# Zeros for the blocks' DRAM tiles come from a constant; attention's output is split between filling pieces

## The chip, the cores and the metric

The kernel runs on one core of one Trainium2 chip. The metric is device time in microseconds (us), the median of three runs. A core has TensorE (PE) for matmuls, with its weight loads (PEld) beside them, VectorE (DVE) and ScalarE (ACT) for elementwise work, GpSimd (POOL), and SyncE (SP), whose queue issues every DMA of this kernel in the order in which they stand in it. Each engine works through its own queue in order and waits on semaphores for what the others produce.

## The reference

One layer of a hybrid block over 256 latent tokens and 256 context tokens, width 2048:

```
sh, sc, g = modulation(cond)                     # silu(cond) @ w_mod + b_mod, for latents and for context
u  = (rmsnorm(x) * (1 + sc) + sh) @ w_in         # one wide projection, its columns are cut into branches
# branch 1: RWKV-7 time mixing, 16 heads of 64, two directions, context first, then latents
#           S = S*w + (S @ -kk) x akk + v x k ;  y = S @ r        (a recurrence over the tokens)
# branch 2: latent attention, 8 heads: softmax(q k^T) v, times silu(zm)
out = x + g * ((g_r * (o_rwkv @ w_br_r) + g_m * (o_mla @ w_br_m)) @ w_out)
```

The recurrence is computed in chunks of 64 tokens, and each chunk needs the inverse of a triangular 64x64 matrix. The inverse of its four 16x16 blocks on the diagonal is computed apart, on 64 partitions, so these blocks travel through DRAM: out of a tile of the chunk, into a narrow tile, and back into a wide one whose other entries must be zero.

## The kernel before

**Precision.** A float32 operand is split into a high part, rounded by ScalarE (`hi`), and a low part, subtracted by VectorE (`lo = src - hi`); a product is three matmuls, `hi*hi`, `hi*lo`, `lo*hi` (`mm3`, L254). `split` (L218) is this pair of operations. Weights come in pieces of 128x512 float32 (`piece`, L234, whose DMA is L237), are split by `parts_of` (L240) and are used by twelve matmuls each. Nearly all elementwise operations are recorded by the profile under one line, L142, and nearly all matmuls under L115, L117 or L120, so groups are told apart by their tiles.

**Stage 1** (to about 136 us): for 16 slices `k` of the width, the modulation weights `wm` (4 x 512 KB for each slice, L296, in 11 buffers), the projection's first six column tiles (`w` from `w_first`, 2 x 192 KB), their splits and their matmuls into the tiles `a`. PE, ACT and DVE have their order written out by hand here (`manual_schedule`).

**Stage 2** (to about 880 us): the recurrence. A main chain of small matmuls runs through `front`, `diagonal` and `back` for each pair of heads. Beside it a generator, `bg`, issues filling pieces: projections of other columns (`proj_g`, L414; weights from `w_proj`), and the matmuls of the output gate on `w_mod_g` (`gate_mm`, L442). A planner in Python (`drive`, L549), which adds up estimated costs of matmuls and elementwise operations, decides after which step of the chain a filling piece is written. DMAs and GpSimd's operations have no cost in it.

**The zeros.** Each of two DRAM tiles, `dw0` and `dw1` (2x8x2x4160 float32), takes the inverted diagonal blocks for a group of heads, and is read back as the wide 64x64 matrices into `WT`. All that isn't a diagonal block has to be zero, and is written once, before stage 2. GpSimd sets the SBUF tile `WT0` to zero (L598), and four DMAs copy it out (L603 and L604, 512 KB and 8 KB for each tile). `WT0` lies in the pool `rw`, in memory that stage 1's pool `p1` used, so the memset waits until that stage's last loads and operations have let go of it. The four DMAs stand in SP's queue between the first two pieces of `w_proj` and the next ones.

**Stage 3** (to about 1117 us): attention, head by head (`attend`, L1362), with filling pieces between its steps; its output is collected in `omla` (128x8x256). The filling pieces here are `branch_g` (L1417), the recurrence's output times `w_br`: for each of 16 column tiles `j` it loads two pieces of weights and a gate tile `th` from DRAM (L1423), does 2 x 12 matmuls into a tile `acc` (two buffers in PSUM), multiplies `acc` by the gate into `th` on VectorE (L1429), which frees `acc`, and stores `th` (L1430). After the last head, `omla` is split into `obh` and `obl` in two halves of 128x1024 (L1452 to L1454). Then twelve steps of `bg` are taken, the pieces' buffers move to the pool `mg`, which is deeper, and the rest of `bg` is run out (L1463). A branch takes three steps of `bg`: one for each piece and one for its end.

**Stage 4** (from about 1117 us): attention's output (`obh`, `obl`) times the other half of `w_br`, into `chp`, merged with the gates, then `w_out`.

**The order on each engine** follows from the code's order by a rule. When the kernel is built, a list scheduler goes through modelled time, and each engine, when it is free, takes from its ready instructions the one that was written first. An instruction that isn't ready is passed over. `high_priority(HP)` in `parts_of` puts the splits of weights 500 places ahead. The order found in this way is then fixed; on the chip each engine keeps to it and waits where its operands aren't there.

Of the kernel before, what the change touches and what calls it, by code (L numbers as in the profile page):

```python
# [16 lines left out]
P = 128  # L17
# [5 lines left out]
CH = 64  # L23
# [7 lines left out]
_CW = [("ident", 128), ("ones", 2), ("mq", 128), ("mr", 128),  # L31
       ("zoff", 128), ("bones", 128), ("hsel", 2),
       ("hmean", 2), ("sel2", 2)]
# [5 lines left out]
NCONST = _o  # L39
# [15 lines left out]
BEHIND = mybir.DependencyInfo(mybir.DependencyClass.NoSync, mybir.DependencyReason.DATA)  # L55
# [6 lines left out]
PD = CH * CH + CH  # L62
# [84 lines left out]
def hybrid_block(  # L147
# [20 lines left out]
    nc = tc.nc  # L168
# [10 lines left out]
    cc = cst.tile([P, NCONST], F32, name="cc")  # L179
    vv = cst.tile([P, NVEC], F32, name="vv")  # L180
    nc.sync.dma_start(vv, vecs)
    nc.sync.dma_start(cc, consts)

    def con(name):
        o, w = CO[name]
# [2 lines left out]
    def vec(name, i, n=1):  # L188
        o, w = VO[name]
        return vv[:, o + i:o + i + n]  # L190
# [27 lines left out]
    def split(src, hi, lo):  # L218

        S.copy(hi, src)  # L220
        V.tensor_tensor(lo, src, hi.bitcast(F32), ALU.subtract)

    def halfs(pool, shape, name, bufs=2):
        return [pool.tile(shape, F32R, name=name + c, tag=name + c, bufs=bufs) for c in "hl"]
# [51 lines left out]
    with tc.tile_pool(name="p1", bufs=2) as p1:  # L276
# [11 lines left out]
        V.memset(ssil, 0.0)  # L288
        V.tensor_scalar(ssil[:, 0:2 * KT], st, 0.5, None, ALU.mult)

        parts, mods = {}, {}

        def load_mod(k):
            for r in range(4):
                wm = p1.tile([P, 4, 256], F32, name="wm", tag="wm", bufs=NWM)
                nc.sync.dma_start(wm, w_mod_ss[k, r])  # L296
                yield wm

        def mod_a(k):

            pm = pp.tile([P, 512], F32, name="pm", tag="ch")
            for r, wm in enumerate(load_mod(k)):
                for g in range(4):
                    k0 = 2 * (4 * r + g)
                    E.matmul(pm[32 * g:32 * g + 32, 0:256], lhsT=ssil[:, k0:k0 + 32], rhs=wm[:, g],
                             start=r == 0, stop=r == 3, tile_position=(0, 32 * g))
            part = p1.tile([P, 256], F32, name="part", tag="part")
            S.copy(part, pm[:, 0:256])
            parts[k] = pm, part

        def mod_b(k):

            pm, part = parts.pop(k)
            for i in range(2):
                E.transpose(pm[:, 256 + 128 * i:384 + 128 * i], part[:, 128 * i:128 * i + 128], ident)
            mod = p1.tile([P, 4], F32, name="mod", tag="mod", bufs=4)
            for i in range(2):
                V.tensor_reduce(mod[:, 2 * i:2 * i + 2],
                                pm[:, 256 + 128 * i:384 + 128 * i].rearrange("p (g c) -> p c g", c=32)[:, 0:2], AX.X, ALU.add)
            V.tensor_scalar(mod[:, 0:2], mod[:, 0:2], vec("bsh", k), None, ALU.add)  # L320
            V.tensor_scalar(mod[:, 2:4], mod[:, 2:4], vec("bsc", k), 1.0, ALU.add, ALU.add)
            V.tensor_scalar(mod[:, 2:4], mod[:, 2:4], vec("norm", k), None, ALU.mult)
            mods[k] = mod
# [3 lines left out]
        for k in range(KT):  # L327
# [5 lines left out]
            g = k % 4  # L333
# [23 lines left out]
        def first(k, half):  # L357
            wh, wl = wks[k][half]
            for i in range(3 * half, 3 * half + 3):
                cs = slice(128 * (i % 3), 128 * (i % 3) + 128)  # L360
                mm3(acc[i], wh[:, cs], wl[:, cs], hmh[:, k], hml[:, k], k == 0, k == KT - 1)
# [3 lines left out]
        def load_first(k):  # L365
            ws[k] = [piece(w_first[k, i], [P, 384]) for i in range(2)]

        def split_first(k):
            wks[k] = [parts_of(w) for w in ws.pop(k)]

        def scale_x(k):
            hxs[k] = p1.tile([P, TT], F32, name="hx", tag="hx")
            V.tensor_tensor(hxs[k], xT[:, k], rsb, ALU.mult)
# [3 lines left out]
        with tc.manual_schedule(engines={mybir.EngineType.PE, mybir.EngineType.Activation, mybir.EngineType.DVE}):  # L377
            scale_x(0)
            for k in range(KT + 1):
                if k < KT:  # L380
                    load_first(k)
                    mod, hx = mods.pop(k), hxs.pop(k)
                    for i in range(2):
                        t0 = slice(T * i, T * i + T)
                        S.activation(hx[:, t0], hx[:, t0], AF.Identity, scale=mod[:, 2 + i:3 + i], bias=mod[:, i:i + 1])
                    split(hx, hmh[:, k], hml[:, k])
                if k > 0:
                    first(k - 1, 0)
                if k + 1 < KT:
                    mod_a(k + 1)  # L390
                    scale_x(k + 1)
                if k < KT:
                    split_first(k)
                if k > 0:
                    first(k - 1, 1)
                if k + 1 < KT:
                    mod_b(k + 1)
        wd = p1.tile([P, TT], F32, name="sq", tag="sq", bufs=4)
        S.activation(wd, acc[0], AF.Tanh)
        split(wd, lrh[:, 0], lrl[:, 0])  # L400
# [194 lines left out]
    with tc.tile_pool(name="rw", bufs=1) as rw:  # L595
        hss = [slice(0, 64), slice(64, 128)]
        WTs = [rw.tile([P, 2, NU, CH], F32, name=f"WT{i}") for i in range(2)]
        nc.gpsimd.memset(WTs[0], 0.0)  # L598
        dws = [dr1.tile([2, 8, 2, PD], F32, name=f"dw{i}") for i in range(2)]
        for t in dws:  # L600
            rows = t.rearrange("w u g (b x) -> (w u g b) x", b=4)
            zero = WTs[0].rearrange("p w u t -> p (w u t)")
            nc.sync.dma_start(rows[:, 0:16 * CH], zero)  # L603
            nc.sync.dma_start(rows[:, 16 * CH:PD // 4], zero[:, 0:PD // 4 - 16 * CH])  # L604


        restart = rw.tile([P, 4 * 65], F32, name="restart")
# [512 lines left out]
        def background():  # L1120

            while main or extra or not closing:
                ready = next((m for m in main if m[0]()), None)
                if ready:
                    main.remove(ready)
                    task = ready[1]
                elif extra:
                    task = extra.pop(0)
                else:
                    yield False  # L1130
                    continue
                for r in task:
                    yield True
                yield True

        closing = False
        bg = background()
# [32 lines left out]
    omla = late.tile([P, 8, T], F32, name="omla")  # L1170
    ob = [[t[:, 8:16, T:TT] for t in (hmh, hml)]]
# [277 lines left out]

    mg = ctx.enter_context(tc.tile_pool(name="mg", bufs=2))  # L1450
    ob.append(halfs(mg, [P, 8, T], "ob", 1))
    for q in range(2):  # L1452
        qs = slice(4 * q, 4 * q + 4)
        split(omla[:, qs], *(t[:, qs] for t in ob[1]))  # L1454

    for _ in range(12):
        next(bg, None)
    place[:] = mg, NWL, NSX, NSX
# [1 line left out]
    def logits():  # L1460
        return mg.tile([P, T], F32, name="th", tag="th", bufs=4)

    for _ in bg:  # L1463
        pass
    while gate_left:
        ps = pp.tile([P, 512], F32, name="acc", tag="acc", bufs=2)
        gate_add(ps[:, 0:T], *gate_mm(ps[:, 0:T]))
# [10 lines left out]
    for j in range(KT):  # L1478
# [8 lines left out]
        t = mg.tile([P, T], F32, name="gt")  # L1487
# [6 lines left out]
    for cb in range(4):  # L1494
# [11 lines left out]
        for i in range(2):  # L1506
# [3 lines left out]
            n = 256 if cb == 3 and i else 512  # L1510
# [7 lines left out]
def _constants():  # L1518
    import numpy as np

    f = np.float32
    c = {}
    c["ident"] = np.eye(P, dtype=f)
    c["ones"] = np.ones((P, 2), f)
    s = np.arange(CH)
    S, Tq = s[:, None], s[None, :]
    two = lambda a, b: np.tile(np.concatenate([a, b], 1).astype(f), (2, 1))
    c["mq"] = two(Tq > S, Tq < S)
    c["mr"] = two(Tq >= S, Tq <= S)
    c["zoff"] = two(S // 16 > Tq // 16, S // 16 < Tq // 16)  # L1530
    h = np.arange(P) // 64
    c["bones"] = (h[:, None] == h[None, :]).astype(f)
    c["hsel"] = (h[:, None] == np.arange(2)[None, :]).astype(f)
    c["hmean"] = c["hsel"] / f(64)
    r = np.arange(P) % 32
    c["sel2"] = (r[:, None] == np.arange(2)[None, :]).astype(f)
    return np.concatenate([c[n].reshape(P, w) for n, w in _CW], 1)


def _rotary():  # L1540
# [11 lines left out]
def _layout(i):  # L1552
# [10 lines left out]
    a["xcT"] = ca(xc.T.reshape(4, 4, P, TT).transpose(0, 2, 1, 3))  # L1563
    a["xn"] = ca(g["x"][0])
    a["consts"] = _constants()
    bm, cv = g["b_mod"][0], g["conv_rkv"][0]
    v = {
# [64 lines left out]
```

## Time and profile before

| | us |
|---|---|
| median of 3 runs | 1258.72 |
| lowest and highest run | 1253.5, 1265.38 |
| the profiled execution's own time | 1256.53 |
| its span, first to last instruction | 1254.7 |

In the profiled execution TensorE is busy for 95% of the span, its weight loads for 80%, VectorE for 75%, ScalarE for 48%; the mean granted clock of TensorE is 0.993. The page gives the span in 40 slices of 31.4 us, the chain of work that ended last (followed back from the last instruction), and groups of instructions. The trace's timeline gives single instructions with their start and duration in us, and in brackets the idle time of the engine before them with what ended it. The windows view gives, for a stretch of time, each engine's busy time, the granted clock of TensorE (PEclk, 1.00 is full speed) and the share of the 16 DMA engines that was busy. "SPq" rows are DMAs as SP issues them; "to landing" is the time from the issue until the data is there.

### The profile page before, as it was taken

The numbers are of one execution on the slowest core, as the hardware profiler recorded it, in microseconds if no ns is written. First come the engines' busy times: TensorE is split into PE (matmuls) and PEld (weight loads), VectorE is DVE, ScalarE is ACT, GpSimd is POOL, SyncE is SP. The second block draws the span as 40 slices with busy tenths as digits, with TensorE's granted clock in tenths as the row PEclk, the third lists the DMA queues.
The fourth block names the chain that finished last, engine by engine and source line by source line (L and its number), as shares of the span: only waits on it lengthen the run. The fifth ranks groups of instructions, "written<-read, shape, count | busy, mean of one in ns | idle before, by whom it ended". The sixth has DMA issues, their size and how long they took to land.

```text
span 1254.7 us, 30101 instructions
## 1 busy us (share of the span) xinstructions
PE 1189.0 (95%) x11613; PEld 1000.5 (80%) x11613; DVE 937.7 (75%) x2642; ACT 596.4 (48%) x1244; POOL 1.9 (0%) x9
## 2 busy tenths in 40 slices
PE   5999998998999999999999899899999999899998
PEld 2665787787877777878887789789899999899886
DVE  4444767868888788888998888865877777768655
ACT  3444542444453454434544456344565656535443
POOL 0000000000000000000000000000000000000000
PEclk9999899999999999999999999999999999999999
DMA  9999447655554455544662655444855433689774
GB/s 377 347 351 352 144 122 180 163 156 146 128 154 126 119 139 136 148 117 124 167 151 62 162 157 146 127 114 142 255 181 152 138 109 115 193 283 295 220 254 139
DMA packets 214127, 222.53 MB, mean 177 GB/s; under 512 B 113168, under 2 KB 138400, under 8 KB 213472
## 3 DMA queue, kind: packets, MB, share of 16 engines
q1 hardware_dynamic: 213984, 220.61, 59.1%
q8 instruction: 91, 1.49, 0.5%
q14 instruction: 52, 0.43, 0.1%
HBM read 201.52 MB, written 19.03 MB: 176 GB/s over the span
## 4 chain that ended last, share of the span: by engine, by line
PE 70%; DMA 15%; DVE 11%; issue 2%; ACT 2%; SPq 0%; DVEq 0%; ACTq 0%
PE acc L120 29%; PE chp L115 11%; PE lv L115 6%; PE acc L117 5%; DMA wm<-in_w_mod_ss 4%; PE a L115 4%; PE ch L115 3%; DMA w<-in_w_proj 3%; DVE wl L142 3%; PE wk L115 2%; PE wk L127 2%; DMA ln<-dl 2%; PE wk L120 2%; PE acc L115 1%; DVE wt L142 1%
## 5 line engine op out<-in xcount | busy, mean ns | idle before, releaser
L142 ACT CAST wh<-w 128x512 fp32r<-128x512 f32 (+1 forms) x484 | 291.0, 608 | 328.4 <-PE acc L120 128.5
L142 DVE TENSOR_TENSOR wl<-w,wh 128x512 fp32r<-128x512 f32 (+1 forms) x480 | 322.6, 675 | 149.6 <-ACT wh L142 77.4
L120 PE MATMUL acc<-hmh,wl 128*128 128x256 f32 (+1 forms) x1312 | 396.7, 302 | 3.9 <-DVE wl L142 3.7
L120 PE MATMUL acc<-hml,wh 128*128 128x256 f32 (+1 forms) x1312 | 394.7, 301 | 0.0
L120 PE MATMUL acc<-hmh,wh 128*128 128x256 f32 (+1 forms) x928 | 273.8, 295 | 0.0
L120 PEld LDWEIGHTS acc<-hmh,wl 128*128 128x128 f32 x1312 | 248.8, 190 | 18.0 <-DVE wl L142 7.0
L120 PEld LDWEIGHTS acc<-hml,wh 128*128 128x128 f32 x1312 | 249.5, 190 | 8.8 <-issue 1.0
L120 PEld LDWEIGHTS acc<-hmh,wh 128*128 128x128 f32 x928 | 176.2, 190 | 5.0
L117 PE MATMUL acc<-hmh,wh 128*128 128x256 f32 (+1 forms) x384 | 146.6, 382 | 7.0 <-DVE th L142 3.5
L117 PEld LDWEIGHTS acc<-hmh,wh 128*128 128x128 f32 x384 | 72.8, 190 | 33.1 <-issue 15.1
L142 DVE TENSOR_TENSOR pr<-wt 64x14 f32<-64x14 f32 (+6 forms) x224 | 42.5, 190 | 2.6
L142 DVE TENSOR_TENSOR wt<-wt,pr 64x14 f32<-64x14 f32 (+6 forms) x224 | 42.3, 189 | 2.2
L115 PE MATMUL a<-hmh,wh 128*128 128x512 f32 x96 | 41.2, 429 | 0.0
L115 PE MATMUL a<-hmh,wl 128*128 128x512 f32 x96 | 38.6, 402 | 0.4 <-DVE wl L142 0.4
L115 PE MATMUL pm<-wm,ssil 128*32 128x256 f32 x512 | 34.5, 386 | 4.4 <-DMA wm<-in_w_mod_ss 4.2
L115 PE MATMUL a<-hml,wh 128*128 128x512 f32 x96 | 38.4, 400 | 0.0
L115 PE MATMUL chp<-obh,wl 128*128 128x256 f32 x128 | 36.2, 283 | 0.0
L115 PE MATMUL chp<-obl,wh 128*128 128x256 f32 x128 | 36.2, 283 | 0.0
L115 PE MATMUL chp<-obh,wh 128*128 128x256 f32 x128 | 36.2, 283 | 0.0
L142 ACT ACTIVATE hx<-hx,mod 128x256 f32<-128x256 f32 x32 | 17.5, 594 | 37.8 <-DVE mod L142 37.8
L142 DVE TENSOR_TENSOR hml<-hx,hmh 128x512 fp32r<-128x512 f32 x16 | 11.1, 693 | 29.0 <-ACT hmh L142 29.0
L115 PEld LDWEIGHTS pm<-wm,ssil 128*32 128x32 f32 x512 | 13.4, 109 | 23.3 <-DMA wm<-in_w_mod_ss 11.5
(347 smaller groups left out, 2223.6 us busy)
## 6 DMA issues: line engine op xcount, KB each, us to landing
w<-in_w_proj SPq DMA_DIRECT2D x296, 256.0 KB, 3.1
wm<-in_w_mod_ss SPq DMA_DIRECT2D x64, 512.0 KB, 7.5
w<-in_w_mod_g SPq DMA_DIRECT2D x64, 256.0 KB, 3.4
w<-in_w_br SPq DMA_DIRECT2D x64, 256.0 KB, 3.9
w<-in_w_out SPq DMA_DIRECT2D x64, 256.0 KB, 3.5
WT<-dw SPq DMA_DIRECT2D x32, 256.0 KB, 4.8
w<-in_w_first SPq DMA_DIRECT2D x32, 192.0 KB, 4.9
thd<-th SPq DMA_DIRECT2D x48, 128.0 KB, 2.9
```

Of the source, the lines that this page charges most:

```text
L115: return self.engine.matmul(out, lhsT=lhsT, rhs=rhs, **kw)
L117: self.head.append(self.engine.matmul(out, lhsT=lhsT, rhs=rhs, **kw))
L120: i = self.engine.matmul(out, lhsT=lhsT, rhs=rhs, **kw)
L127: return self.engine.transpose(*a)
L142: return fn(out, *a, **kw)
```

## The change

Two edits.

1. The array of constants gets 1040 more columns, all zero. Each of the two `dw` tiles is now filled by one DMA from these columns, DRAM to DRAM, 128 rows of 4160 bytes; the memset of `WT0` and the four DMAs from it are gone. Each new DMA is put behind the last load of the modulation weights `wm` in the order (`add_manual_dep` with `BEHIND`, an edge of order without a semaphore).
2. The two halves of the splitting of `omla` are no longer written ahead of the twelve steps of `bg`, but inside the loop that runs out the rest of it: one half after its fourth step, one after its eighth. Counted in branches, the first stands behind the end of the fifth branch after attention, the second behind the first piece of the seventh. The twelve steps before the pool changes stay.

```diff
-    nc.sync.dma_start(cc, consts)
+    nc.sync.dma_start(cc, consts[:, 0:NCONST])
...
-        parts, mods = {}, {}
+        parts, mods, loads = {}, {}, []
...
-                nc.sync.dma_start(wm, w_mod_ss[k, r])
+                loads.append(nc.sync.dma_start(wm, w_mod_ss[k, r]))
...
+        last_load = loads[-1]
...
-        nc.gpsimd.memset(WTs[0], 0.0)
         dws = [dr1.tile([2, 8, 2, PD], F32, name=f"dw{i}") for i in range(2)]
         for t in dws:
-            rows = t.rearrange("w u g (b x) -> (w u g b) x", b=4)
-            zero = WTs[0].rearrange("p w u t -> p (w u t)")
-            nc.sync.dma_start(rows[:, 0:16 * CH], zero)
-            nc.sync.dma_start(rows[:, 16 * CH:PD // 4], zero[:, 0:PD // 4 - 16 * CH])
+            z = nc.sync.dma_start(t.rearrange("w u g (b x) -> (w u g b) x", b=4), consts[:, NCONST:NCONST + PD // 4])
+            tc.add_manual_dep(z.ins, last_load.ins.name, BEHIND, reason="zeros")
...
     ob.append(halfs(mg, [P, 8, T], "ob", 1))
-    for q in range(2):
-        qs = slice(4 * q, 4 * q + 4)
-        split(omla[:, qs], *(t[:, qs] for t in ob[1]))
-
     for _ in range(12):
         next(bg, None)
     place[:] = mg, NWL, NSX, NSX
...
-    for _ in bg:
-        pass
+    halves_ = [slice(4 * q, 4 * q + 4) for q in range(2)]
+    for n, _ in enumerate(bg):
+        if n % 4 == 3 and halves_:
+            qs = halves_.pop(0)
+            split(omla[:, qs], *(t[:, qs] for t in ob[1]))
+    for qs in halves_:
+        split(omla[:, qs], *(t[:, qs] for t in ob[1]))
...
-    return np.concatenate([c[n].reshape(P, w) for n, w in _CW], 1)
+    return np.concatenate([c[n].reshape(P, w) for n, w in _CW] + [np.zeros((P, PD // 4), f)], 1)
```

## The prediction

> **What bounds the kernel.** I read the page first, its head, part 1 and the chain of work that ended last.
>
> ```profile
> span 1254.7 us, 30101 instructions
> PE 1189.0 (95%) x11613; PEld 1000.5 (80%) x11613; DVE 937.7 (75%) x2642; ACT 596.4 (48%) x1244; POOL 1.9 (0%) x9
> PE 70%; DMA 15%; DVE 11%; issue 2%; ACT 2%; SPq 0%; DVEq 0%; ACTq 0%
> ```
>
> TensorE is the bound: 95% busy, 70% of the chain. So an edit pays only where it closes a gap of PE or where PE runs slower than it could. Both edits touch a short stretch, so I read the windows view there (columns: stretch, length, busy us of PE, PEld, DVE, ACT, POOL, granted clock, DMA share, GB/s).
>
> ```profile
> 120.00:125.00 5.00, 5.00 (x42) 3.53 (x44) 2.06 (x8) 2.24 (x5) 0.00 (x0) 1.00 0.92 349
> 125.00:130.00 5.00, 5.00 (x36) 3.70 (x29) 2.87 (x9) 1.73 (x5) 0.00 (x0) 1.00 0.24 68
> 135.00:140.00 5.00, 5.00 (x40) 3.99 (x39) 5.00 (x9) 4.31 (x8) 1.32 (x3) 1.00 0.62 234
> 140.00:145.00 5.00, 3.24 (x19) 2.87 (x18) 4.87 (x17) 2.05 (x4) 0.00 (x0) 0.73 0.76 234
> 145.00:150.00 5.00, 5.00 (x24) 4.73 (x23) 2.96 (x10) 1.36 (x3) 0.00 (x0) 0.59 0.44 135
> 1090.00:1095.00 5.00, 1.78 (x16) 1.53 (x15) 4.91 (x8) 2.84 (x6) 0.00 (x0) 0.96 0.88 272
> 1095.00:1100.00 5.00, 5.00 (x31) 5.00 (x32) 2.59 (x5) 2.48 (x4) 0.00 (x0) 0.70 0.95 317
> ```
>
> Right behind the zeros (140 to 150) and right behind attention's splits (1090 to 1100) PE first stands and then has a low clock. These are the two places.
>
> **The zeros, as they are.** SP's, POOL's, PE's and ACT's timelines:
>
> ```profile
> 120.73 1.83 SPq L237 DMA_DIRECT2D w<-in_w_first  x2
> 136.36 0.33 SPq L603 DMA_DIRECT2D dw<-WT  x1
> 138.04 0.46 SPq L604 DMA_DIRECT2D dw<-WT  x1
> 138.60 1.75 SPq L237 DMA_DIRECT2D w<-in_w_proj  x3
> 135.37 0.96 POOL L598 MEMSET WT<- 128x1024 f32 x1 [134.44 <-DMA w<-in_w_proj]
> 136.59 0.64 PE L115 MATMUL acc<-w,ssil 128*32 128x256 f32 x8
> 140.10 0.95 PE L115 MATMUL wk<-cc,sq 128*128 128x2 f32 x8
> 142.57 0.58 PE L117 MATMUL acc<-hmh,wh 128*128 128x256 f32 x1 [1.53 <-ACT wh L142]
> 143.59 0.58 PE L120 MATMUL acc<-hmh,wl 128*128 128x256 f32 x1 [0.23 <-DVE wl L142]
> 141.90 0.62 ACT L142 CAST wh<-w 128x512 fp32r<-128x512 f32 x1 [2.39 <-DMA w<-in_w_proj]
> ```
>
> The memset ends at 136.33, the first zero DMA goes at 136.36, the last (L604) at 138.04, and only then the next weights, at 138.60. ACT gets them at 141.90, PE at 142.57, after 1.53 us idle and 0.23 more for the low part.
>
> Without these DMAs, what holds the weights back? Their buffers: the gate's eight matmuls at 136.59 read the tiles that they replace. Half of the eight free the first tile at about 136.9. So the issue moves from 138.60 to 136.9, 1.7 us earlier, and the first piece lands 3.3 us later as it does now (138.60 to 141.90), or 3.1 as the median of its kind, the page's part 6:
>
> ```profile
> w<-in_w_proj SPq DMA_DIRECT2D x296, 256.0 KB, 3.1
> ```
>
> That is 140.0 to 140.2 us; with the cast's 0.62 the high part is there at 140.6 to 140.8, before PE comes free at 142.57 - 1.53 = 141.04. The low part needs DVE, which is full here (5.00 of 5.00, then 4.87); but splits of weights go 500 places ahead, so it starts behind one running operation, at about 140.9, and ends 0.7 us later, where PE's third matmul wants it at 141.3. I leave 0.3 us of stall: 1.53 + 0.23 - 0.3 = 1.5 us saved.
>
> The clock: 0.73 and 0.59 over 5 us each cost 5 x 0.27 + 5 x 0.41 = 3.4 us. Ahead of the drop, from 140.10 to 142.57, PE had nothing but eight two-column matmuls and the gap. Without the gap I expect no drop, as elsewhere PE works on at 1.00. The edit is worth 1.5 + 3.4 = 4.9 us.
>
> The Trainium skill, TensorE: Matmul & The Clock Gate (Part 1, The HAM clock gate), says that the clock is halved after one idle window of 3.4 us and restored after a busy one. By that rule a stall of 1.53 us cannot do it, and the sum for this edit would be 1.5 us; the trace, with 0.73 and 0.59 behind 1.53 us, so far disagrees.
>
> **The zeros, as they will be.** Two DMAs of 128 x 4160 B = 0.53 MB each are put behind the last `wm` load. SP's queue is free there until 120.73, so they may stand ahead of the last `w_first` pieces. No row shows a copy from DRAM to DRAM. The nearest is the SBUF-to-DRAM copy of the same zeros, 2.9 us for 512 KB; at the 349 GB/s of 120 to 125 both would take 1.06 MB / 0.349 = 3.1 us, twice that (6.1) if reading and writing count apart.
>
> ```profile
> dw<-WT SPq DMA_DIRECT2D x2, 512.0 KB, 2.9
> w<-in_w_first SPq DMA_DIRECT2D x2, 192.0 KB, 4.2
> 131.12 0.92 ACT L142 CAST wh<-w 128x384 fp32r<-128x384 f32 x2
> ```
>
> The last first-stage weights land at 120.73 + 4.2 = 124.9 (the second, issued within that row's 1.83 us, up to 1.8 later) and are cast from 131.12 on. Behind the zeros they land at 128.0 to 131.0, the second at 129.8 to 132.8, wanted at 131.6. I take 3.1 us, nearest to the measured copy, and so no cost; the cover is the empty DMA stretch 125 to 130 (share 0.24). If it is gone, up to 1.2 us. The zeros themselves are done earlier than now, so no reader of `dw` waits longer. On SP the two also pass the loads of `wup`, of the gate's weights and of the first `w_proj`, all of which are issued behind the idle stretch; POOL loses its memset and keeps two short ones, for which nobody waits in the views. The load of the constants keeps its 128 rows, now cut out of longer ones: nothing.
>
> **Attention's splits.** DVE's order, then PE:
>
> ```profile
> 1088.83 0.69 DVE L142 TENSOR_TENSOR wl<-w,wh 128x512 fp32r<-128x512 f32 x1 [1.04 <-PE acc L120]
> 1089.44 1.22 DVE L142 TENSOR_TENSOR obl<-omla,obh 128x1024 fp32r<-128x1024 f32 x1
> 1091.17 1.22 DVE L142 TENSOR_TENSOR obl<-omla,obh 128x1024 fp32r<-128x1024 f32 x1
> 1092.31 2.07 DVE L142 TENSOR_TENSOR wl<-w,wh 128x512 fp32r<-128x512 f32 x3
> 1094.30 0.74 DVE L142 SCALAR_TENSOR_TENSOR th<-th,acc 128x256 f32<-128x256 f32 x2
> 1088.57 0.28 PE L117 MATMUL acc<-hmh,wh 128*128 128x256 f32 x1
> 1094.86 0.55 PE L117 MATMUL acc<-hmh,wh 128*128 128x256 f32 x1 [3.22 <-DVE th L142]
> 1085.07 0.33 SPq L1423
> th<-thd SPq DMA_DIRECT2D x16, 128.0 KB, 2.6
> ```
>
> PE stands 3.22 us for `th`, which frees an `acc` (L1429). The first of these two operations had its operands early: its gate tile was loaded at 1085.07 + 2.6 = 1087.7, and PE began the next branch at 1088.57. It runs at 1094.30 because it was written behind the two `obl` and three `wl` go ahead of both. Written ahead of the splits, `th` follows the `wl` of 1088.83, at 1089.4, and `acc` is free long before 1091.64. Waste: 3.22 of stall and 5 x 0.04 + 5 x 0.30 = 1.7 of clock, 4.9 in all.
>
> Not all comes back. ACT's casts keep their order and wait for loads:
>
> ```profile
> 1096.07 0.62 ACT L142 CAST wh<-w 128x512 fp32r<-128x512 f32 x1 [2.26 <-DMA w<-in_w_br]
> 1096.92 1.28 ACT L142 CAST wh<-w 128x512 fp32r<-128x512 f32 x2 [0.23 <-DMA w<-in_w_br]
> 1100.59 0.28 PE L117 MATMUL acc<-hmh,wh 128*128 128x256 f32 x1
> 1089.15 3.86 DMA w<-in_w_br
> 1116.85 46.06 PE chp L115 x384
> ```
>
> A matmul takes 46.06 / 384 = 0.12 us, a piece of twelve 1.4 us. From 1091.64 the fourth piece would start at 1095.9, against 1100.59 now: 4.7 us. But its weights are the second cast of 1096.92; where that order stays, it starts at about 1097.6, and 3.0 us are left. I take 3.5. The splits (two of 1.22 us on DVE, their casts ahead of them on ACT) must now find room before 1116.85; DVE was busy 2.59 of 5 us in 1095 to 1100, so they cost nothing there, and 1.2 us each at most if they delay a `wl`. From 1116.85 the chain is PE alone, so the gain reaches the end.
>
> **Sum.** 4.9 + 3.5 = 8.4 us, from 1256.53 to 1248.1 for a profiled execution. The median shown, 1258.72, lies 2.2 above that one, so I predict 1250. The runs of before spread over 12 us, 0.95%: a measurement tells about 1% from no change, that is 12.6 us.
>
> **Rivals.**
>
> *The clock stays low.* The light work around the gap (eight two-column matmuls, eight matmuls of 32 columns) may drop it by itself. The first edit then gives 1.5, the second 2.0: 1255. For it: the drop after 1.53 us; against it: the eight of 32 columns lie in a stretch (135 to 140) at 1.00.
>
> *Loads bound the second place.* The chain of waits there shows no `ob` at all: it runs through the load at 1089.15, 3.86 long, into the cast, `wl` and `th`. If `th` stays behind that third `wl`, the second edit gives nothing: 1254. Against it: `th` needs nothing of this load.
>
> *The order changes for the worse: slower.* Loads that come 1.7 us earlier in the scheduler's modelled time shift which instruction is ready first, and the order of 700 us of stage 2 follows. The chain there already holds late loads:
>
> ```profile
> 183.90 3.21 DMA w<-in_w_proj
> 197.68 4.03 DMA w<-in_w_proj
> ```
>
> One more costs about 3.6 us, and with a clock drop (1.7) 5.3. Two of them use up the 8.4; from the second on the kernel is slower, with three 1258.7 - 8.4 + 15.9 = 1266, and 1% slower from four. The same lottery can take such waits away: two fewer give 1240 to 1243.
>
> *It does not do what it says.* If the splits fill the same idle slots of DVE and `th` still comes late, and the `w_first` pieces lose 1.2 behind the zeros, some 4 us of the first place are left or less: 1255 to 1259.
>
> **How the numbers follow.** Forecast (1244 to 1256 by its bounds) 0.48; clock 0.14; loads 0.14; worse order 0.12; better order 0.07; nothing done 0.05. The range takes all but the tails of the two orders: 1242 to 1263. Faster by over 1% means under 1246.1: the low end of the forecast (0.11) and the better order (0.07), 0.18. Slower means above 1271.3: half of the worse order, 0.06. Within: 0.76.
>
> **What would show it.** No L598 or L603 rows; two DRAM-to-DRAM DMAs at about 118 us; `w_proj` issued at about 137; no PE gap over 0.5 us at 141 and a clock of 1.00 from 140 to 150. At the end of attention, `th` ahead of both `obl`, no gap of 3 us, `chp` beginning 3 to 5 us nearer to attention's last matmul than now. Wrong it is if the clock still drops at 140 with no gap there, or if stage 2 is longer or shorter by more than 4 us between the same two pieces.

## The result and the profile after

The changed kernel takes 1248.06 us (median of 6 runs, 1241.94 to 1251.79), beside 1259.16 for the kernel before in the same session (6 runs). The ratio is 0.9906, with a 95% interval of 0.9878 to 0.9933: some 12 us, and surely a gain. The profiled execution took 1251.79 us, the slowest of its six. One execution of `zeros_only` below took 1873.44 us, far from all others, and is left out of its numbers.

The page of the changed kernel: its head, part 1 and the chain of work that ended last.

```profile
span 1250.0 us, 30096 instructions
PE 1191.2 (95%) x11613; PEld 1003.0 (80%) x11613; DVE 936.7 (75%) x2642; ACT 596.6 (48%) x1244; POOL 1.0 (0%) x8
PE 64%; DVE 16%; DMA 15%; issue 3%; ACT 2%; SPq 1%; DVEq 0%; ACTq 0%
```

The work is the same; only the time between is less. The windows view at the two places (columns as in the prediction; stage 1 ended 2.2 us later in this execution, the last matmul into `a` standing at 138.43 here and at 136.27 before):

```profile
125.00:130.00 5.00, 5.00 (x45) 2.96 (x44) 1.85 (x3) 2.88 (x6) 0.00 (x0) 1.00 0.93 331
140.00:145.00 5.00, 5.00 (x45) 4.94 (x44) 4.77 (x8) 3.11 (x6) 0.00 (x0) 1.00 0.78 232
145.00:150.00 5.00, 5.00 (x28) 4.24 (x27) 4.94 (x18) 2.67 (x6) 0.00 (x0) 1.00 0.58 189
1085.00:1090.00 5.00, 4.37 (x36) 4.09 (x36) 3.99 (x7) 2.88 (x5) 0.00 (x0) 1.00 0.83 260
1090.00:1095.00 5.00, 4.81 (x42) 4.62 (x41) 3.52 (x7) 2.50 (x5) 0.00 (x0) 1.00 0.92 300
1095.00:1100.00 5.00, 3.49 (x23) 3.11 (x23) 2.69 (x5) 0.72 (x2) 0.00 (x0) 0.88 0.73 237
1100.00:1105.00 5.00, 5.00 (x36) 5.00 (x36) 1.83 (x4) 1.69 (x3) 0.00 (x0) 0.78 0.57 167
```

The copies fill the DMA engines from 125 to 130 (share 0.93, 0.24 before). From 140 to 150 PE is full and at full speed (3.24 of 5 us at 0.73 before, then 0.59). Behind attention one hole of 3.22 us has become several small ones, and the clock falls there still. The timelines at the first place, SP, ACT and PE:

```profile
122.72 1.83 SPq L237 DMA_DIRECT2D w<-in_w_first  x2
124.60 1.25 SPq L601 DMA_DIRECT2D dw<-in_consts  x2
139.41 1.75 SPq L237 DMA_DIRECT2D w<-in_w_proj  x4
141.97 1.35 ACT L142 CAST wh<-w 128x512 fp32r<-128x512 f32 x2 [0.59 <-DMA w<-in_w_proj]
143.03 0.36 PE L117 MATMUL acc<-hmh,wh 128*128 128x256 f32 x1
```

The next `w_proj` goes out 139.41 - 138.43 = 0.98 us after the last `a`, against 138.60 - 136.27 = 2.33 before, and PE takes its piece without a wait. DVE and PE at the second place:

```profile
1084.75 0.41 DVE L142 SCALAR_TENSOR_TENSOR th<-th,acc 128x256 f32<-128x256 f32 x1
1085.08 1.22 DVE L142 TENSOR_TENSOR obl<-omla,obh 128x1024 fp32r<-128x1024 f32 x1
1090.33 0.42 DVE L142 SCALAR_TENSOR_TENSOR th<-th,acc 128x256 f32<-128x256 f32 x1
1090.66 1.22 DVE L142 TENSOR_TENSOR obl<-omla,obh 128x1024 fp32r<-128x1024 f32 x1
1089.26 0.39 PE L120 MATMUL acc<-hmh,wl 128*128 128x256 f32 x1 [0.63 <-DVE wl L142]
1096.33 0.39 PE L120 MATMUL acc<-hmh,wl 128*128 128x256 f32 x1 [0.63 <-DVE wl L142]
1098.65 0.39 PE L117 MATMUL acc<-hmh,wh 128*128 128x256 f32 x1 [0.87 <-PE acc L120]
1158.95 0.50 PE L115 MATMUL ch<-wh,mh 128*128 128x512 f32 x1 [0.35 <-DVE gt L142]
```

`th` now runs ahead of each `obl`, and other waits follow, one of them in stage 4 (1158.95), where there was none.

To see where the time went I cut each profile at the same instructions and asked the windows view for the stretches between. First the kernel before, then the changed one: from the last matmul into `a` to the 33rd group `chp<-xs,W` (**stretch A**, the first quarter of stage 2), from the last `chp<-hmh,vfl` to the first `chp<-obh,wh` (**stretch B**, attention's end), and from there to the last matmul (**stage 4**).

```profile
136.27:313.70 177.43, 164.56 (x1552) 137.68 (x1550) 133.54 (x384) 75.87 (x156) 0.42 (x3) 0.97 0.57 155
1087.05:1116.69 29.64, 26.17 (x209) 25.68 (x207) 17.61 (x29) 12.43 (x20) 0.00 (x0) 0.94 0.86 272
1116.69:1249.77 133.08, 133.08 (x769) 117.87 (x768) 92.17 (x173) 62.88 (x109) 0.00 (x0) 1.00 0.74 240
```

```profile
138.43:307.62 169.19, 160.85 (x1553) 134.70 (x1551) 133.55 (x384) 75.26 (x156) 0.00 (x0) 0.99 0.57 156
1082.37:1111.47 29.10, 26.77 (x209) 25.92 (x207) 16.84 (x28) 11.65 (x19) 0.00 (x0) 0.94 0.77 243
1111.47:1245.22 133.75, 133.40 (x770) 117.93 (x768) 91.87 (x173) 63.92 (x110) 0.00 (x0) 1.00 0.76 246
```

Length less PE's busy time is its idle time: 12.9 us in stretch A before and 8.3 after, 3.5 and 2.3 in stretch B. Stretch A is 8.2 us shorter, stretch B 0.5, stage 4 is 0.7 longer. So the gain lies in the first stretch, over 170 us, and not only at 142. Elsewhere this execution lost some: the granted clock was halved for 6.8 us at 914, which it wasn't before.

**What a length is made of.** The trace's record of the granted clock gives stretches at half speed. If I take from a length its idle time and half of its half-speed time, stretch A leaves 158.4 to 160.1 us in all fourteen profiles of this study, and stage 4 leaves 133.1 to 133.4. So, to within 1.7 us, two kernels differ in idle time and in clock only, and these two are what the experiments are read by.

### The profile page after: what moved, and what is told of

Same layout as the page of the kernel before. It is cut to its first block, busy times and chain, and to the rows that moved or that the text cites. A ratio compares the mean times of both kernels' runs of the same rounds, so it can differ in the third digit from the quotient of the medians.

```text
span 1250.0 us, 30096 instructions
## 1 busy us (share of the span) xinstructions
PE 1191.2 (95%) x11613; PEld 1003.0 (80%) x11613; DVE 936.7 (75%) x2642; ACT 596.6 (48%) x1244; POOL 1.0 (0%) x8
## 4 chain that ended last, share of the span: by engine, by line
PE 64%; DVE 16%; DMA 15%; issue 3%; ACT 2%; SPq 1%; DVEq 0%; ACTq 0%
PE acc L120 25%; PE chp L115 9%; PE lv L115 6%; PE acc L117 5%; DVE wl L142 4%; DMA wm<-in_w_mod_ss 4%; PE a L115 4%; PE ch L115 3%; DMA w<-in_w_proj 3%; PE wk L115 2%; PE wk L127 2%; PE wk L120 2%; DVE wt L142 2%; DMA ln<-dl 2%; PE acc L115 1%
## 5 line engine op out<-in xcount | busy, mean ns | idle before, releaser
L117 PEld LDWEIGHTS acc<-hmh,wh 128*128 128x128 f32 x384 | 72.4, 189 | 29.0 <-issue 11.7
L142 DVE TENSOR_TENSOR hml<-hx,hmh 128x512 fp32r<-128x512 f32 x16 | 11.1, 692 | 29.0 <-ACT hmh L142 29.0
L115 PEld LDWEIGHTS pm<-wm,ssil 128*32 128x32 f32 x512 | 13.9, 110 | 23.4 <-DMA wm<-in_w_mod_ss 10.6
```

The lines of the kernel that those rows point to most:

```text
L115: return self.engine.matmul(out, lhsT=lhsT, rhs=rhs, **kw)
L117: self.head.append(self.engine.matmul(out, lhsT=lhsT, rhs=rhs, **kw))
L142: return fn(out, *a, **kw)
```

## The experiments

The theories: PLACE, which is the prediction's (each edit pays where it stands: 4.9 and 3.5 us); ORDER (the zeros' edit pays because stage 2 gets another order); CLOCK (the half-speed stretches come by chance); LOADS (behind attention, waits for loads take the place of the wait for `th`). The results stand in this table, each with the ratio to the kernel before on the same chip, and lengths and idle times of PE as in the two fences above.

| kernel | median us | ratio, 95% interval | A: us, idle | half speed in A, us | B: us, idle | stage 4 us |
|---|---|---|---|---|---|---|
| before | 1259.16 | 1 | 177.4, 12.9 | 10.2 | 29.6, 3.5 | 133.1 |
| after | 1248.06 | 0.9906 (0.9878 to 0.9933) | 169.2, 8.3 | 3.4 | 29.1, 2.3 | 133.7 |
| after_again | 1250.71 | 0.9912 (0.9882 to 0.9942) | 169.8, 8.6 | 3.4 | 27.7, 2.4 | 134.2 |
| zeros_only | 1251.64 | 0.9921 (0.9893 to 0.9949) | 169.8, 9.1 | 3.4 | 29.8, 3.5 | 133.1 |
| splits_only | 1258.02 | 0.9987 (0.9963 to 1.0011) | 179.2, 15.5 | 10.2 | 27.3, 2.6 | 134.3 |
| small_pair | 1253.25 | 0.9937 (0.9912 to 0.9961) | 169.6, 8.5 | 3.4 | 30.4, 4.2 | 133.1 |
| order_back | 1260.83 | 1.0008 (0.9986 to 1.0030) | 175.6, 13.9 | 3.4 | 31.4, 3.9 | 133.1 |
| rnb_first | 1255.82 | 0.9977 (0.9953 to 1.0001) | 173.7, 12.0 | 3.4 | 30.1, 3.9 | 133.1 |
| three | 1253.12 | 0.9938 (0.9917 to 0.9959) | 173.9, 11.7 | 7.4 | 26.4, 1.3 | 133.1 |
| zeros_ahead | 1246.12 | 0.9897 (0.9870 to 0.9924) | 169.8, 8.6 | 3.4 | 27.7, 2.7 | 133.6 |
| th_first | 1255.25 | 0.9974 (0.9957 to 0.9990) | 174.8, 12.3 | 6.8 | 27.8, 1.8 | 133.7 |
| th_eight | 1247.77 | 0.9914 (0.9887 to 0.9942) | 169.5, 8.8 | 3.4 | 27.3, 2.4 | 133.4 |
| zeros_th | 1247.51 | 0.9897 (0.9865 to 0.9929) | 171.0, 8.8 | 6.8 | 26.6, 1.7 | 133.2 |
| both_th | 1247.99 | 0.9897 (0.9868 to 0.9926) | 170.1, 7.6 | 6.8 | 28.4, 2.5 | 135.0 |

The half-speed column is summed from the trace's clock record; the kernel before stood at 1258.5 to 1260.6 in the later sessions.

### The two edits apart

`zeros_only` is the change without the move of the splits; `splits_only` is that move alone; `after_again` is the changed kernel once more. `zeros_only` against the changed kernel, and `splits_only` against the kernel before:

```diff
+    for q in range(2):
+        qs = slice(4 * q, 4 * q + 4)
+        split(omla[:, qs], *(t[:, qs] for t in ob[1]))
...
-        if n % 4 == 3 and halves_:
...
+        pass
```

```diff
-    for q in range(2):
-        qs = slice(4 * q, 4 * q + 4)
-        split(omla[:, qs], *(t[:, qs] for t in ob[1]))
...
+        if n % 4 == 3 and halves_:
+            qs = halves_.pop(0)
+            split(omla[:, qs], *(t[:, qs] for t in ob[1]))
```

> The first edit alone; attention's splits stay where they were. Three theories. PLACE (the prediction's): the edit pays at the start of stage 2 only, 4.9 us by the sum, so a time of about 1254.3; PE's idle time from the last matmul into `a` to the 33rd group `chp<-xs,W` (12.9 us before) falls by 1.5. ORDER: the matmuls of stage 2 stand in another order, and stalls at 190 to 313 us go away with it; idle time in that stretch falls to about 8.3 as in the changed kernel, 1251 to 1253. CLOCK: stretches at half clock come by chance, each 3.4 us long, wherever PE happened to be idle for about 40% of a stretch of that length; where they lie differs from run to run, and the clock is worth 1.7 us for each, not 3.4 for certain. ORDER and CLOCK can both hold.

> The second edit alone: everything ahead of attention's end stands in the order of before. PLACE: 3.5 us, so 1255.7, with the stretch from the last `chp<-hmh,vfl` to the first `chp<-obh,wh` 26.1 us long (29.6 before, of which 3.5 are idle and 1.7 are lost to a half clock). Rival, LOADS: the 3.22 us behind `th` turn into several waits for `wl`, for `w` and for `th`'s own load, as the profile of the changed kernel has them (2.3 us idle there); then the edit gives 1.2 us of idle time and now and then a half clock of 1.7, so 1257 to 1258.

> The changed kernel once more, beside its parts: 1248 within 2 us. Idle time of PE by stretch as in its first profile, within 0.5 us where the order is fixed (8.3 from the last `a` to the 33rd `chp<-xs,W`, 21.1 to the last of these, 2.3 from the last `chp<-hmh,vfl` to the first `chp<-obh,wh`). PLACE expects the clock to stay at full speed from 140 to 150 and to fall where it fell in the first profile (at 709, 914 and 1099); CLOCK expects the half-clock stretches to lie elsewhere.

The zeros' edit gives 0.79% (9.9 us, 6.4 to 13.5) and the move of the splits 0.13% (1.6 us, from a loss of 1.4 to a gain of 4.7). Together that is 11.5, and the changed kernel measured 0.88% (11.1) beside them. So nearly all of the gain is the zeros'. PLACE's 4.9 us for them is too little; ORDER's forecast of idle time in stretch A (8.3) came out at 9.1, its 1251 to 1253 at 1251.64. For the splits, LOADS was right in its numbers: 2.6 us idle and 1258.

In the changed kernel's first profile the half-speed stretches lie at 30, 85, 215, 710, 914 and 1099 us, in its second at 210, 384, 473, 544 and 916. Two of these places are the same (215 and 210, 914 and 916, at the same matmuls), the others are not. So CLOCK is half right: half speed returns at some places, and chance decides whether it comes there. The place 74 to 81 us behind the last `a`, at 215 here, has one in twelve of the fourteen profiles; another, 339 to 351 us behind it, in nine.

### Without the 512-KB copies, but with the memset

```diff
+        nc.gpsimd.memset(WTs[0], 0.0)
...
+            z = nc.sync.dma_start(rows[:, 0:16 * CH], consts[:, NCONST:NCONST + 16 * CH])
+            tc.add_manual_dep(z.ins, last_load.ins.name, BEHIND, reason="zeros")
+            nc.sync.dma_start(rows[:, 16 * CH:PD // 4], zero[:, 0:PD // 4 - 16 * CH])
```

> The first edit, but the memset of `WT0` stays, and the two DMAs of 8 KB that read it stay in SP's queue behind the first two `w_proj`, ahead of the next; only the two of 512 KB come from the constants. The order of stage 2's matmuls is then near that of before (388 lines differ, 1549 with the whole first edit). If it was the wait for the memset that held the weights back, PE still stands 1.5 us at 142. If it was the issuing of four DMAs (136.36 to 138.50, 2.1 us, against 0.9 for two), the next `w_proj` goes about 1.2 us earlier and the gap is under 0.5 us. PLACE expects the whole 4.9 us, 1254.3; ORDER expects the stalls of before at 190 to 313 us to stay (idle time from the last `a` to the 33rd `chp<-xs,W` about 11 us, not 8.3), and 1255.5 to 1257.

The count of lines in this expectation misleads: most of them differ only in the numbers of buffers. Without these, the order of PE differs from that of before in 106 rows and from that of `zeros_only` in none. So it has the new order, and it can't speak on ORDER. On the wait it does (SP's timeline):

```profile
136.87 0.80 SPq L606 DMA_DIRECT2D dw<-WT  x2
137.78 1.79 SPq L237 DMA_DIRECT2D w<-in_w_proj  x4
```

With the last `a` at 136.79, the weights go 0.99 us later, as without the memset, and no gap is left at 142 (the first PE wait over 0.3 us stands at 186.55). The memset was still there, so it was the issuing of four DMAs (136.36 to 138.50) that held the weights back, not the wait for it.

### The zeros' edit with the old order

Pieces that were written behind the first transposes of `rnb` (the reciprocal norms of the first pair's keys) may no longer pass them, from the fifth burst on. (A burst is six or twelve matmuls of a piece that stay together.)

```diff
+            return self.stand(self.head[-1])
...
+    def stand(self, i):
+        if self.behind is not None:
+            self.since += 1
+        if self.since > 4:
+            self.tc.add_manual_dep(i.ins, self.behind.ins.name, BEHIND, reason="order")
+        return i
...
+                tr = E.transpose(ps[:, 128 * i:128 * i + 128], rnb[:, 128 * i:128 * i + 128], ident)
+            E.behind = E.behind or tr
```

> The first edit alone, with the order of stage 2's matmuls as it was before: pieces written behind the first four transposes of `rnb`, from the fifth burst on, may not be placed ahead of them. With buffer numbers left out, PE's order is then that of before in every row (the first edit alone moves 106 rows). PLACE (the weights' earlier arrival alone is worth the gain): idle time from the last `a` to the 33rd `chp<-xs,W` 9 us or less, as with the new order, and a time within 1.5 us of the 1251.7 of the first edit. ORDER (the rest of the gain comes from the pieces' new places): the gap at 142 is gone, but the later stalls of before (191 to 235 us and at 313) stay, idle time 10.5 to 13.5 us, 1254 to 1257.

All of the gain is gone: 1.0008, at most 0.14% by the interval. So the earlier weights alone are worth nothing. (The reverse, the new order with the four DMAs of before, was not run.) The gap at 142 is not there, as the prediction had it, and it is not saved either. DVE and PE of the kernel before, of this one and of `zeros_only`, at the first `rnb`, with the windows view of stretch A for the last two:

```profile
147.60 0.43 DVE L142 COPY rnb<-rn 128x512 f32<-128x512 f32 x1
150.15 0.60 PE L127 MATMUL wk<-cc,rnb 128*128 128x128 f32 x4
```

```profile
148.17 0.43 DVE L149 COPY rnb<-rn 128x512 f32<-128x512 f32 x1
148.66 0.66 PE L127 MATMUL wk<-cc,rnb 128*128 128x128 f32 x4 [3.82 <-DVE rnb L149]
135.64:311.22 175.58, 161.68 (x1553) 134.88 (x1551) 133.13 (x384) 75.50 (x156) 0.00 (x0) 0.99 0.55 151
```

```profile
145.99 0.43 DVE L142 COPY rnb<-rn 128x512 f32<-128x512 f32 x1
147.66 0.60 PE L127 MATMUL wk<-cc,rnb 128*128 128x128 f32 x4
132.98:302.81 169.83, 160.77 (x1553) 134.69 (x1551) 133.67 (x384) 75.86 (x156) 0.00 (x0) 0.99 0.57 156
```

Before, `rnb` is ready 11.8 us after the last `a` (147.60 + 0.43 - 136.27) and PE comes 2.1 us later. With the weights earlier and the old order, `rnb` is ready after 13.0 us, but PE is free at 144.84 and waits 3.82 us. VectorE was full already (5.00 and 4.87 of 5 us in the prediction's windows): now one more low part of the weights, a copy and two passes into `cr`, which came behind `rnb` before, stand ahead of it. In `zeros_only` four more bursts of six 128x512 matmuls stand ahead of `rnb`: by its rule the scheduler passes over what isn't ready. A matmul of that size takes 0.23 us (the step between two of them), so these are 24 x 0.23 = 5.5 us of work, and they cover the wait. Later stalls count too: behind the first 16 us of the stretch PE idles 11.1 us in the kernel before, 10.1 here and 9.1 in `zeros_only`.

### The old order, with `rnb` earlier

Is VectorE's queue what makes `rnb` late? Six convolution passes are put behind it.

```diff
+            if taps == "cv" and j < 2 or taps == "ck" and j == 1:
+                convs.append(i)
...
+            while convs:
+                tc.add_manual_dep(convs.pop().ins, last.ins.name, BEHIND, reason="rnb")
```

> As the last run but one (first edit alone, stage 2's matmuls in the order of before), where PE stood 3.82 us at 148.66 for VectorE's `rnb`; now six convolution passes of VectorE (`cv` of two heads, `ck` of the second, 0.66 us each, 4 us in all) stand behind `rnb` in its order, where they stood ahead. ORDER, with VectorE as what is late next: `rnb` comes about 3.5 to 4 us earlier, the gap at 149 is under 1 us, idle time from the last `a` to the 33rd `chp<-xs,W` falls from 13.9 to 10 or 11, and the time by 3.5 to 5.5 us with the clock, to 1254 to 1256. Rival: `rnb` waits for its own chain of thirteen small operations and for PE's two-column matmuls, not for the passes ahead of it; then the gap stays above 2.5 us and the time at about 1259.5.

VectorE around `rnb`, and stretch A:

```profile
147.30 0.42 DVE L149 COPY rnb<-rn 128x512 f32<-128x512 f32 x1
147.63 0.74 DVE L149 SCALAR_TENSOR_TENSOR cv<-a,vv,cv 128x510 f32<-128x510 f32 x1
137.89:311.63 173.74, 161.76 (x1553) 134.62 (x1551) 133.49 (x384) 75.42 (x156) 0.00 (x0) 0.99 0.56 152
```

It is. `rnb` comes 9.8 us after the last `a` (137.89), 3.1 earlier than in `order_back`, and PE no longer waits for it. The 1.9 us less of idle time is not the whole 3.82: the wait at the stretch's end is 2.83 us here (at 311.63) and 0.62 in `order_back`. In time, 1255.82 is 0.31% (3.9 us) below `order_back` by the ratios, but the two intervals overlap, so this gain is not clear of noise. From `order_back` to `zeros_only` it is 0.87%: covering this one wait does not bring back the whole gain.

### A new draw of the order

The same six passes behind `rnb`, now with the zeros' edit as it is (and `th` put ahead as below).

> The first edit with `th` put ahead behind attention (as in the run before last) and the six convolution passes behind `rnb` (as where the order of before was kept). PE does not wait for `rnb` at 148 with the new order, so by that place alone there is nothing to gain: 1247.5, within 1.5 us. But the order of stage 2 is drawn anew (101 rows of PE's order differ). ORDER, as the runs so far have it: idle time from the last `a` to the 33rd `chp<-xs,W` was 12.0 to 15.5 us with the order of before and 7.6 to 9.1 with the new one, so a new draw may move the time by up to 5 us either way, 1243 to 1252; `th`'s stretch stays at 26 to 28.5 us.

PE at the end of stretch A, and the stretch:

```profile
307.56 0.37 PE L115 MATMUL chp<-xs,W 64*64 64x64 f32 x2 [3.37 <-DVE xs L142]
133.69:307.56 173.87, 162.13 (x1552) 135.22 (x1550) 133.32 (x384) 75.34 (x156) 0.00 (x0) 0.98 0.55 152
```

An edit that looks harmless at its place costs 0.41% (5.2 us, by the two intervals 0.4 to 10) against `zeros_th`, and 1253.12 lies a little above the 1252 that I had allowed: idle time in stretch A is 11.7 again, and the same group that waited 2.03 us in the kernel before (at 313.70), 0.97 in the changed one (at 307.62), waits 3.37. Stretch B keeps its 26.4 us. So the order of stage 2 by itself can be worth some 5 us, of which stretch A, 2.9 us longer, shows about half.

### Where the copies stand in SP's queue

The prediction had them ahead of the last two `w_first`; they stand behind. Here they are put ahead, by a priority.

```diff
-            z = nc.sync.dma_start(t.rearrange("w u g (b x) -> (w u g b) x", b=4), consts[:, NCONST:NCONST + PD // 4])
+            with tc.high_priority(5000):
+              z = nc.sync.dma_start(t.rearrange("w u g (b x) -> (w u g b) x", b=4), consts[:, NCONST:NCONST + PD // 4])
```

> The changed kernel with the two copies of zeros ahead of the last two loads of `w_first` in SP's queue, where the prediction had put them; in the changed kernel they stand behind these. Every other order is the same. The two landed 5.9 and 6.5 us after their issue in the changed kernel's first profile, beside the last `wm`. The prediction: the loads come 3.1 us later, 6.1 at most, which the idle queue covers; no cost, or 1.2 us at most: 1248 to 1251. Rival, TRAFFIC: the copies slow the last `wm` and `w_first` more than that, PE waits for `wh` at about 131, and it is 1251 to 1253.

```profile
115.27 1.93 SPq L602 DMA_DIRECT2D dw<-in_consts  x2
117.67 1.84 SPq L237 DMA_DIRECT2D w<-in_w_first  x2
```

The first of these two loads now lands at 126.07, 8.4 us after its issue; in `zeros_only`, with the copies behind it, 4.5 us (117.45 to 121.94). So the two copies cost the load about 4 us, between the 3.1 and the 6.1 that I had as ends, and stage 1 shows none of it: the last `a` stands at 134.01, in `after_again` at 133.90. TRAFFIC falls; 1246.12 is the lowest median of all, but not to be told from 1248.06.

### Behind attention: `th` first, with the splits left alone

```diff
+            with late[0](HP):
                 V.scalar_tensor_tensor(th, th, 1.0, ps[:, 0:T], ALU.add, ALU.mult)
...
     ob.append(halfs(mg, [P, 8, T], "ob", 1))
+    late[0] = tc.high_priority
```

`th_first` does this to the kernel before, `zeros_th` to `zeros_only`, `both_th` to the changed kernel.

> The kernel before, with attention's splits where they were; only the multiplications into `th` behind attention are put 500 places ahead, as the splits of weights are. That is the step that the prediction gave for the second edit (`th` stood behind both `obl`). PLACE: the 3.22 us ahead of 1094.86 are gone or under 1 us, the stretch from the last `chp<-hmh,vfl` to the first `chp<-obh,wh` falls from 29.6 to about 26, no half clock there, 1255 to 1256. LOADS: other waits of 2 us or more in sum stand in that stretch (for `w`, for `wl`, for `th`'s load), 27 to 28.5 us, 1257 to 1258.5, as with the splits moved.

> The first edit with attention's splits left where they were ahead of the twelve steps, and the multiplications into `th` behind attention put 500 places ahead. If `th`'s place is what counts, and not the splits', the stretch from the last `chp<-hmh,vfl` to the first `chp<-obh,wh` is about 26 us without a half clock (27.8 with one, 1.8 us idle), as where the same was done to the kernel before: 1247 to 1249. If the splits on VectorE delay the weights' low parts there, 27.3 us or more and 1249 to 1251.

> The changed kernel with the multiplications into `th` behind attention put 500 places ahead. If the waits left in that stretch (2.3 us) come from `th` behind the low parts of weights, 1.8 us idle or less and 0.5 to 1 us off the time, 1246.5 to 1248. If they come from weights that land late, 2.3 us idle as before and no change, 1248 to 1249.5.

Stretch B of `splits_only`, of `th_first` and of `zeros_th`:

```profile
1097.72:1125.07 27.35, 24.79 (x208) 24.32 (x207) 16.81 (x28) 11.79 (x19) 0.00 (x0) 1.00 0.78 246
```

```profile
1089.10:1116.87 27.77, 25.97 (x209) 25.68 (x208) 16.66 (x28) 11.59 (x19) 0.00 (x0) 0.94 0.80 247
```

```profile
1079.52:1106.12 26.60, 24.94 (x208) 24.36 (x207) 16.41 (x28) 11.69 (x19) 0.00 (x0) 1.00 0.81 250
```

`th`'s place is indeed the cause of the 3.22 us: with nothing moved but `th`, idle time falls from 3.5 to 1.7 or 1.8 (1.3 in `three`), and `th_first` gains 0.26% (3.3 us, 1.3 to 5.4). Moving the splits does the same by a longer way and leaves more: 2.3 to 2.7 us idle in five profiles, and 0.4 to 1.2 us more in stage 4 (133.4 to 134.3 against 133.1). Both together are no better than either (`both_th` 2.5 idle, 135.0 in stage 4). In whole times, `zeros_th` (1247.51) and the changed kernel can't be told apart.

### What is left behind attention

```diff
-        return mg.tile([P, T], F32, name="th", tag="th", bufs=4)
+        return mg.tile([P, T], F32, name="th", tag="th", bufs=8)
```

> The changed kernel with eight buffers for `th` behind attention where it has four; every engine's order stays as it is. In its profile SP waits 4.4 us in five places from 1080 to 1112 until a store `thd<-th` has landed, because the next load `th<-thd` writes the same buffer, and the weights stand behind that load. LOADS: these waits hold up the loads behind them; with eight buffers the idle time of 2.3 us in the stretch falls under 1.2, 1 us or a little more off the time. PLACE, in which that idle time is due to the splits' two passes on VectorE: no change (2.3 us idle). Rival: SP waits 6.0 us for `th` itself ahead of its stores, and that stays: then 1.5 to 2.3 us idle.

No change: 2.4 us idle. But SP's waits for the stores to land only fell from 4.4 to 2.5 us, so the run says no more than that these 1.9 us cost nothing that PE feels. Whether the waits that are left, SP's waits for `th` itself, or the loads' own time make up the idle time was not tried and stays open.

## Why the prediction was right, and where it was not

Predicted 1250 with 1242 to 1263, and within 1%; measured 1248.06 and -0.94%. The number is right, in part by luck: of the two terms behind it one was too small and one too large, and the larger gain came by a way that the forecast did not have.

1. **The weights go earlier, and the gap at 142 closes.** Right. The issue moved by 2.33 - 0.98 = 1.35 us (1.7 predicted); no profile with the edit has the gap (`rnb_first` and `three` wait 0.64 us there, for a low part). `small_pair` shows that it was the four DMAs, as the prediction had it, and not the memset.
2. **"The edit is worth 1.5 + 3.4 = 4.9 us."** This step failed as it stands. It stopped at the gap and did not ask what is late next. That is `rnb`, on the very VectorE that I had quoted as full: with the order kept, the gap moves to it, grown to 3.82 us, and the edit is worth nothing (`order_back`). What the gain needs is a better order, the mechanism of the rival to which I gave 0.07; but that rival's time, 1240 to 1243, did not come, since it was reckoned on top of gains that are not there by themselves. In stretch A the eight profiles with the edit and the new order average 169.8 us, with 8.6 us idle and 4.3 at half speed; the three that have both the order of before and its four DMAs (before, `splits_only`, `th_first`) average 177.1, 13.5 and 9.1. So the edit is worth 7.3 us there, 5.0 of idle time and 2.4 of clock. The gap and its drop, which I had priced at 4.9, make 1.9 and 2.8 of this: with the new order the size came out, though not by the way that I gave. The other 3.1 us of idle time lie behind the gap, where the forecast had nothing, and 0.4 of clock is lost again there.
3. **The clock.** The drop at 142 was there in all three profiles with the gap, twice for 6.8 us and once for 3.4, and in no profile without it (`order_back` has one at 150, behind its 3.82 us); that much was right. But a place has a chance of a drop, not a fixed price; more on it below.
4. **The copies.** They stand behind the last `w_first`, not ahead of it as I had it. They land 5.9 and 6.5 us after their issue, slower than the 3.1 that I took for both, and cost nothing in either position, as predicted: the cover that I named held.
5. **"I take 3.5" for the splits (3.0 to 4.7).** The mechanism was right: `th` at 1084.75 stands ahead of both `obl`, and `th_first` shows it alone. The size was off. Stretch B averages 27.8 us in the five profiles with the splits moved and 30.3 in the five in which nothing there is changed: 2.5 us, and 0.8 are given back in stage 4. That leaves 1.7, as `splits_only`'s median has it. What I had named as the limit, casts that wait for loads, took more than I allowed (in the changed kernel the casts at 1087.26 and 1090.21 waited 1.03 and 1.29 us for `w`, and PE waited for the low parts behind the first at 1089.26); and "they cost nothing there", of the splits in their new place, is wrong by the waits in stage 4.
6. **The rivals.** "The clock stays low" did not come: no profile without the gap has a drop there. "Loads bound the second place" was half right: `th` did move ahead, but waits of 2.3 us replace it. "The order changes for the worse" did not come with this edit; that it could is shown by `three`, with 5.6 us.

7. **The signs.** `chp` was to begin 3 to 5 us nearer to attention's last matmul; it began 0.5 nearer in this profile and 2.5 on average. The prediction was also to be wrong if stage 2 became shorter or longer by more than 4 us between the same two pieces. It did not say which; stretch A became 8.2 us shorter, where 4.9 were forecast, so the sign did show that something other than the gap had moved.

7.3 and 1.7 make 9.0 of the 11 to 12 us. The rest lies in stage 1, which ends at 133.0 to 138.4 us (134.7 on average) in the eight profiles and at 136.3 to 139.2 (137.3) in the three. Most of it is there already when the last `wm` load is issued, ahead of the copies (115.9 and 118.2 on average). Ahead of that the change touches only the load of the constants, the two ranges overlap, and no run here tells whether it is chance. The long stretch from A to B adds nothing to it: 776.4 us in the eight and 776.9 in the three, though single profiles run from 772.8 to 782.2.

## What to carry to other kernels

When a wait at a stage's start goes, follow the chain one engine further before counting it: if the engine that was waiting meets another full one a few microseconds later, the gain is only what other work can be put in between. Where a scheduler fixes the order, a local edit draws a new order for all that follows; keep the old order on purpose in one experiment, or the local reason will be credited with what the order did. And cut the profiles at the same instructions and compare idle time and clock by stretch: medians alone could not have told these terms apart.

## What the runs showed of the hardware

**The clock is halved by the window, and half a window idle is enough.** Within one execution the half-speed stretches are 3.4 us long or a multiple, and start on one grid: in the kernel before at 29.6, 142.3 and 234.4 us, and (142.3 - 29.6) / 3.413 = 33.0, (234.4 - 142.3) / 3.413 = 27.0. I cut all fourteen profiles into these windows, from 30 to 1236 us, and took for each window at full speed the share in which a matmul was running. Under 0.5, 30 of 31 windows were followed by half speed; from 0.5 to 0.6, 12 of 34; from 0.6 to 0.75, 12 of 171; from 0.75 to 0.9, 4 of 419; above, none of 4212. So a stall of 1.5 to 2 us can halve the clock, or not, by where it falls on a grid that each execution lays anew: a wait of 1.9 us for `rnb`, 74 to 81 us behind the last `a`, stands in all fourteen profiles, and half speed comes with it in twelve. Each halving costs up to half of a window, 1.7 us. The Trainium skill, TensorE: Matmul & The Clock Gate (Part 1, The HAM clock gate), has the free-running window of 3413 ns, and the grid agrees with it. I had read its "idle window" as one without work; the runs show that half is enough, and so the 1.5 us that I gave as this rule's sum for the first edit was a misreading.

**Matmuls of two columns hardly count as work.** In the changed kernel the profile has PE busy through all of the window at 914.5 us, and the next one was at half speed too. But nearly half of that window is this row:

```profile
916.42 1.70 PE L115 MATMUL wk<-ones,sqk 128*128 128x2 f32 x8
```

Of 79 half-speed windows 18 were followed by another, nine of them with PE busy throughout. If the time of two-column matmuls (each from its start to the next one's) is taken out of the share, all 13 with a share under 0.8 were followed by another, of those from 0.8 to 0.9 it was 4 of 8, and above that 1 of 58. At full speed the same share parts the windows better too: under 0.45, 33 of 33 were followed by half speed; from 0.45 to 0.6, 21 of 67; from 0.6 up, 4 of 4767, where it was 16 of 4802 with these matmuls counted. The window ahead of the drop at 142 (from 138.9) has 0.64 with them and 0.36 without, so the eight at 140.10 had a part in it beside the gap. No run changes these matmuls alone, so this is read from the fourteen profiles and not tested. The same page of the Trainium skill has the clock come back after one busy window; the runs agree where the window holds real work.
